# An elementwise GELU on one core: the first two loads put ahead of SyncE's register set-up

## Chip, cores, metric

The kernel runs on one core of one Trainium2 chip. The metric is device microseconds of the whole execution. Executions within 1.5% of the fastest of the same kernel count as fast.

## The reference

```python
# x, y: float32 [1024, 4096]
z = x + y
return 0.5 * z * (1 + np.tanh(np.sqrt(2 / np.pi) * (z + 0.044715 * z ** 3)))
```

33.55 MB are read and 16.78 MB written, with a handful of elementwise operations for each element.

## The kernel before

x and y come in four pairs of loads of 4 MB each, all issued by SyncE (SP below). GpSimd (POOL) and VectorE (DVE) add, ScalarE (ACT) squares and takes the sigmoid, VectorE multiplies, and three stores leave by the same queue. What matters here is the head of the program. Ahead of the kernel's body stands a head block in which each engine sets up its registers and all of them meet at a barrier. The kernel edits this block after its own schedule is made: it takes the first two loads out of the body and puts them ahead of SyncE's drain at the barrier, so that they need not wait for it.

```python
def begin_early(nc, count):
    blocks = nc.main_func.blocks
    head, body = blocks[0], blocks[1]
    SP = mybir.EngineType.SP
    queue = [i for i in body.instructions if i.engine == SP]
    moved = [i for i in queue if isinstance(i, mybir.InstDMACopy)][:count]
    assert not any(i.sync_info and i.sync_info.on_wait for i in moved)
    at = next(k for k, i in enumerate(head.instructions) if i.engine == SP and isinstance(i, mybir.InstDrain))
    for k, i in enumerate(moved):
        body.instructions.remove(i)
        head.instructions.insert(at + k, i)

# ... (at the end of the kernel)
    ctx.close()
    tc.close()
    tc.compile()
    begin_early(nc, 2)
    wait_late(nc)
```

`wait_late` edits the end of the program and is the same in both kernels. After these edits the launch code finishes the program in one more pass over all instructions, and hands it to the compiler. At the time of the edit the SyncE part of the head reads: a register set to zero, a base address loaded into two registers, four registers of bounds, [the two loads], drain, barrier, branch.

Of the kernel before, what the change touches and what calls it, by code (L numbers as in the profile page):

```python
# [10 lines left out]
def begin_early(nc, count):  # L11


    blocks = nc.main_func.blocks
    head, body = blocks[0], blocks[1]
    SP = mybir.EngineType.SP
    queue = [i for i in body.instructions if i.engine == SP]
    moved = [i for i in queue if isinstance(i, mybir.InstDMACopy)][:count]
    assert not any(i.sync_info and i.sync_info.on_wait for i in moved)
    at = next(k for k, i in enumerate(head.instructions) if i.engine == SP and isinstance(i, mybir.InstDrain))  # L20
    for k, i in enumerate(moved):
        body.instructions.remove(i)
        head.instructions.insert(at + k, i)


def wait_late(nc):
# [43 lines left out]
def kernel(  # L70
# [159 lines left out]
# [5 lines that stand above are left out]
# [29 lines left out]
```

## Time and profile before

| | before |
|---|---|
| time, median of the first 3 runs | 120.31 us (120.29 to 120.60) |
| span of the profiled run (120.49 us) | 118.8 us |
| DMA queue's share of 16 engines | 98.7% |
| busiest compute engine | VectorE, 62% |

The span runs from the first recorded instruction to the last. The zero of a profile's clock is therefore that first instruction, whichever it is. "SPq" is SyncE's sequencer; the duration of a DMA row there is the issue, not the transfer (0.38 us for the first load). The lines themselves stand in the prediction.

### The profile page before, as it was taken

The numbers are of one execution on the slowest core, as the hardware profiler recorded it, in microseconds if no ns is written. First come the engines' busy times: TensorE is split into PE (matmuls) and PEld (weight loads), VectorE is DVE, ScalarE is ACT, GpSimd is POOL, SyncE is SP. The second block draws the span as 40 slices with busy tenths as digits, with TensorE's granted clock in tenths as the row PEclk, the third lists the DMA queues.
The fourth block names the chain that finished last, engine by engine and source line by source line (L and its number), as shares of the span: only waits on it lengthen the run. The fifth ranks groups of instructions, "written<-read, shape, count | busy, mean of one in ns | idle before, by whom it ended". The sixth has DMA issues, their size and how long they took to land.

```text
span 118.8 us, 172 instructions
## 1 busy us (share of the span) xinstructions
DVE 73.7 (62%) x35; ACT 61.0 (51%) x34; POOL 69.7 (59%) x19
## 2 busy tenths in 40 slices
DVE  0000000635799995739999968999994999990000
ACT  5000000063888965197698647888839779810000
POOL 0000000699996099999959999959999990000000
DMA  7989898989999898989899898998899889999996
GB/s 243 463 375 507 353 529 353 507 375 474 408 419 463 375 507 353 518 364 496 386 452 430 386 496 353 529 529 353 353 596 463 353 353 441 441 441 441 397 397 265
DMA packets 1584, 50.33 MB, mean 424 GB/s; under 512 B 176, under 2 KB 176, under 8 KB 176
## 3 DMA queue, kind: packets, MB, share of 16 engines
q1 hardware_dynamic: 1584, 50.33, 98.7%
HBM read 33.55 MB, written 16.78 MB: 424 GB/s over the span
## 4 chain that ended last, share of the span: by engine, by line
DMA 51%; POOL 26%; POOLq 4%; DVE 4%; DVEq 2%; ACT 2%; issue 0%; SPq 0%
DMA y<-in_y_dram 51%; POOL z L153 26%; POOLq L231 4%; DVE w L164 2%; DVEq L231 2%; DVE z L176 2%; ACT w L158 2%; SPq L129 0%; POOLq L153 0%
## 5 line engine op out<-in xcount | busy, mean ns | idle before, releaser
L153 POOL TENSOR_TENSOR z<-z,y 128x2048 f32<-128x2048 f32 x15 | 69.4, 4660 | 28.3 <-DMA y<-in_y_dram 28.3
L158 ACT ACTIVATE w<-z 128x2048 f32<-128x2048 f32 x16 | 30.1, 1882 | 37.7 <-DVE z L153 21.5
L164 DVE SCALAR_TENSOR_TENSOR w<-w,z 128x2048 f32<-128x2048 f32 x16 | 36.7, 2296 | 11.2 <-ACT w L158 11.0
L176 DVE TENSOR_TENSOR z<-w,z 128x2048 f32<-128x2048 f32 (+1 forms) x17 | 35.9, 2155 | 0.0
L169 ACT ACTIVATE w<-w 128x2048 f32<-128x2048 f32 x16 | 29.7, 1855 | 4.4 <-DVE w L164 4.3
L153 DVE TENSOR_TENSOR z<-z,y 128x2048 f32<-128x2048 f32 x1 | 2.3, 2293 | 20.5 <-DMA y<-in_y_dram 20.5
L216 ACT ACT_TABLE_LOAD x1 | 1.3, 1283 | 1.3 <-PEq L248 1.3
L215 DVE MEMSET one<- 128x1 f32 x1 | 0.1, 59 | 1.3 <-PEq L248 1.3
L248 POOL MEMSET const-float32-0.0<- 128x1 f32 x1 | 0.1, 98 | 0.2 <-issue 0.2
L216 ACT ACTIVATE one<-one 128x1 f32<-128x1 f32 x1 | 0.2, 203 | 0.0
L248 POOL MEMSET const-bfloat16-1.0<- 128x1 bf16 x1 | 0.1, 101 | 0.0
L248 POOL MEMSET const-uint8-127<- 128x1 uint8 x1 | 0.1, 101 | 0.0
L248 POOL MEMSET const-float32-1.0<- 128x1 f32 x1 | 0.1, 98 | 0.0
## 6 DMA issues: line engine op xcount, KB each, us to landing
z<-in_x_dram SPq DMA_DIRECT2D x4, 4096.0 KB, 31.4
y<-in_y_dram SPq DMA_DIRECT2D x4, 4096.0 KB, 22.2
out_dram<-z SPq DMA_DIRECT2D x1, 5120.0 KB, 15.8
out_dram<-z SPq DMA_DIRECT2D x1, 3072.0 KB, 11.9
out_dram<-z SPq DMA_DIRECT2D x1, 22.0
```

What stands on the lines that cost most here:

```text
L153: eng.tensor_add(out=zt[:, a:b], in0=zt[:, a:b], in1=yt[s][:, o : o + b - a])
L158: nc.scalar.activation(out=wt[c], in_=zt[:, a:b], func=act.Square, scale=root)
L164: nc.vector.scalar_tensor_tensor(out=wt[c], in0=wt[c], scalar=c1, in1=zt[:, a:b], op0=alu.add, op1=alu.mult)
L169: nc.scalar.activation(out=wt[c], in_=wt[c], func=act.Sigmoid)
L176: ins = nc.vector.tensor_mul(out=zt[:, a + o : a + o + n], in0=wt[c][:, o : o + n], in1=zt[:, a + o : a + o + n],)
L215: nc.vector.memset(one, 0.0)
L216: nc.scalar.activation(out=one, in_=one, func=act.Sigmoid)
L231: tc.compile()
L248: nc = _bacc.Bacc("TRN2", target_bir_lowering=False, num_devices=1)
```

## The change

The intent: nothing at all should stand ahead of the two loads on SyncE. They use no register, as a new assertion makes sure, so they need not wait for the register set-up.

```diff
 def begin_early(nc, count):
-    blocks = nc.main_func.blocks
-    head, body = blocks[0], blocks[1]
+    head, body = (b.instructions for b in nc.main_func.blocks[:2])
     SP = mybir.EngineType.SP
-    queue = [i for i in body.instructions if i.engine == SP]
-    moved = [i for i in queue if isinstance(i, mybir.InstDMACopy)][:count]
+    moved = [i for i in body if i.engine == SP and isinstance(i, mybir.InstDMACopy)][:count]
     assert not any(i.sync_info and i.sync_info.on_wait for i in moved)
-    at = next(k for k, i in enumerate(head.instructions) if i.engine == SP and isinstance(i, mybir.InstDrain))
+    assert all(i.regs_accessed() == ((), ()) for i in moved)
+    at = next(k for k, i in enumerate(head) if i.engine == SP)
     for k, i in enumerate(moved):
-        body.instructions.remove(i)
-        head.instructions.insert(at + k, i)
+        body.remove(i)
+        head.insert(at + k, i)
```

## The prediction

Its sum came to 0 instructions removed and 0 added, 0.00 us, and so to the time of before. The 0.4 us of the intent now rest on the second estimate alone, 6 x 60 ns = 0.36 us.

> **What bounds the kernel now.** I read the page top down: busy shares, slices, DMA queue, then the chain of waits, the SyncE rows of the timeline, and SyncE's waits. The page first:
>
> ```profile
> span 118.8 us, 172 instructions
> DVE 73.7 (62%) x35; ACT 61.0 (51%) x34; POOL 69.7 (59%) x19
> ...
> DMA  7989898989999898989899898998899889999996
> GB/s 243 463 375 507 353 529 353 507 375 474 408 419 463 375 507 353 518 364 496 386 452 430 386 496 353 529 529 353 353 596 463 353 353 441 441 441 441 397 397 265
> ...
> q1 hardware_dynamic: 1584, 50.33, 98.7%
> HBM read 33.55 MB, written 16.78 MB: 424 GB/s over the span
> ```
>
> No compute engine is busy for more than 62% of the span. The DMA engines are: the one queue's packets take 98.7% of what 16 engines could give, and every slice between the first and the last has a DMA digit of 8 or 9. 50.33 MB over 118.8 us is the 424 GB/s of the last line. So this kernel is a transfer of a fixed 50.33 MB, and its length is: how late the transfer starts, plus bytes over rate, plus the end. The change aims at the first of the three. The first slice is visibly the thinnest of the early ones, 243 against 463 GB/s; in slices of 118.8/40 = 2.97 us that is some (463 - 243)/463 x 2.97 = 1.4 us of transfer missing at the start (an estimate, since neighbouring slices swing between 353 and 529).
>
> The chain of waits, which the page gives by line and another answer by time, begins so:
>
> ```profile
> 1.20 0.07 issue
> 1.26 0.33 SPq L129
> 1.59 0.05 issue
> 1.64 39.62 DMA y<-in_y_dram
> ```
>
> It starts not at the first pair of loads but at the second, issued at 1.26 and 1.64 us; the fourth load of the queue takes 39.62 us from issue to landing because it stands behind the 12 MB before it. These two issues come after the barrier of the kernel's head, and they are early enough: they queue behind the 8 MB of the first pair. So it is the first pair that sets when the queue begins to move. The beginning of the timeline:
>
> ```profile
> 0.00 0.38 SPq L129 DMA_DIRECT2D z<-in_x_dram  x1
> 0.23 0.10 POOL L248 MEMSET const-float32-0.0<- 128x1 f32 x1 [0.23 <-issue]
> ...
> 0.43 0.42 SPq L136 DMA_DIRECT2D y<-in_y_dram  x1
> 1.26 1.28 ACT L216 ACT_TABLE_LOAD   x1 [1.26 <-PEq L248]
> 1.26 0.33 SPq L129 DMA_DIRECT2D z<-in_x_dram  x1
> 1.33 0.06 DVE L215 MEMSET one<- 128x1 f32 x1 [1.33 <-PEq L248]
> 1.64 0.48 SPq L136 DMA_DIRECT2D y<-in_y_dram  x1
> ```
>
> This is the row to look at: the load of x is the first thing in the span, at 0.00. Nothing recorded of any engine is ahead of it, neither a SyncE instruction nor Pool's first constant at 0.23 us. In SyncE's list of waits no wait precedes either load; its first is of 0.2 us on the barrier:
>
> ```profile
> SPq L248 <- PEq L248: 0.2, 1, 0.2
> ```
>
> The profile does not show everything that is on the clock: the profiled run took 120.49 us and its span is 118.80, so 1.69 us of the time are outside the span. If instructions of SyncE ran unrecorded ahead of its first load, they would be in that part.
>
> [...] the first issue shows 0.38 us, while the median landing of x is 31.4 us after its issue. [...] No row of the trace shows a register instruction[...].
>
> **The change, part by part.** At the time when the kernel edits its own instruction list, the head of SyncE reads: a register set to zero, a base address loaded into two registers, four registers of bounds set, then the two loads (placed there already by the kernel before), then a drain and a wait of the barrier. The new code puts the two loads ahead of the six set-up instructions; an added assertion says that the loads use no register. The two loads' own waits, semaphores, sizes and order stay. Nothing else is added, removed or moved.
>
> What those six would cost if they ran, as estimates. [...] From the trace instead: SyncE's small instructions at the end of the kernel follow one another at about 60 ns (starts at 111.58, 111.64, 111.71 and 111.76 us), so 6 x 60 = 0.36 us. All of it would be on the path, since the queue would start that much earlier and is full ever after. So the intent is worth 0.4 us in 120.3, 0.3%.
>
> But I also built both kernels and compared what comes out. The instruction list is finished after the kernel's edits, and in the finished program of the kernel before, SyncE has no register set-up any more: its 30 instructions are 11 DMA issues, 13 semaphore instructions, 4 drains and 2 branches. The set-up is dropped as unused in both kernels. Engine by engine, the two programs are the same instructions in the same order, and the five engines' binary streams are the same byte for byte; only line numbers in the debug information differ, as the function is one line shorter. The trace of before fits: it has 28 records of SyncE, 11 DMA issues, 13 semaphore instructions and 4 drains, which is the finished list without its branches. So the cost removed is 0 instructions x anything = 0. Added: 0. The sum is 0.00 us, and the prediction is the time of before within its scatter.
>
> **The rivals.** First, the intent as written: the set-up runs and the loads overtake it; 0.4 us gained, about 119.9 us. For it: the 1.69 us outside the span, in which unrecorded instructions could lie. Against it: the finished program has none of them. Even if the whole 1.69 us were set-up, the time would be 118.6 us, 1.4% less and still within 2%.
>
> Second, something that SyncE needs is now not set when the first loads are issued, and they run slower, or with another split over the engines. For it: only that the source puts them ahead of a base load. Against: the same bytes are issued from the same place in the binary. It would cost time in proportion to 8 MB of 50, if at all; I give it almost nothing.
>
> Third, the loads do start earlier but the gain is hidden: the barrier ends at 1.2 us anyway, and the second pair waits for it. This would give 0 as well, but by a wrong reason: with the queue at 98.7% the first pair's start, not the barrier, sets the end.
>
> Fourth, another chip or another placement of the tensors: this moves the same program by its scatter. Three runs of before lie between 120.29 and 120.60, 0.26%, and the profiled one at 120.49.
>
> **Range and chances.** The middle is the median of before, 120.31; I say 120.33, a little above, because the runs scatter upwards (two at 120.3, one at 120.6, one at 120.49). The range is 119.95 to 120.75: it allows for somewhat more than the scatter seen on each side, and its lower end just takes in the first rival. Over 2% faster would need 117.9 us, more than all that is outside the span; over 2% slower 122.7 us, seven times the scatter. I give each 1%, and 98% to the same.
>
> **What would show it.** Right: a span near 118.8 us with the load of x at 0.00, the load of y at about 0.43 and the second pair at about 1.26 and 1.64 us; 172 instructions, again 28 of SyncE; 98 to 99% of the queue; a time outside the span of again 1.5 to 1.8 us. The distances inside the head are the test: with an identical binary they can move by some tens of ns alone. Wrong: if Pool's first constant or the barrier stood later relative to the load of x by 0.3 us or more, SyncE's first load would have moved against the other engines, so there was a set-up to overtake, and the first rival holds; if the first loads' landing times grew by more than a microsecond, the second does. And a repeated run of both on one chip that differs by more than 0.5% between the medians would say that identical streams are not all that decides.

## The result

The changed kernel takes 120.36 us (median of 6, 120.32 to 120.44), the kernel before 120.39 us (median of 6 runs, 120.29 to 120.60). The ratio is 0.9997, with a 95% interval of 0.9984 to 1.001: the same. Here and below a ratio compares the fast runs of the two kernels in the same rounds; it is not quite the ratio of the medians.

The page of the changed kernel:

```profile
span 118.8 us, 172 instructions
...
q1 hardware_dynamic: 1584, 50.33, 98.8%
HBM read 33.55 MB, written 16.78 MB: 424 GB/s over the span
```

Its chain of waits by time (start us, us, what), the first pieces:

```profile
1.20 0.07 issue
1.26 0.33 SPq L128
1.59 0.05 issue
1.64 39.59 DMA y<-in_y_dram
```

Its timeline, from the start:

```profile
0.00 0.38 SPq L128 DMA_DIRECT2D z<-in_x_dram  x1
0.23 0.10 POOL L247 MEMSET const-float32-0.0<- 128x1 f32 x1 [0.23 <-issue]
...
0.43 0.42 SPq L135 DMA_DIRECT2D y<-in_y_dram  x1
1.26 1.28 ACT L215 ACT_TABLE_LOAD   x1 [1.26 <-PEq L247]
1.26 0.33 SPq L128 DMA_DIRECT2D z<-in_x_dram  x1
...
1.64 0.49 SPq L135 DMA_DIRECT2D y<-in_y_dram  x1
```

Line by line these are the rows of before, one source line further up. The load of x is at 0.00, Pool's first constant 0.23 us behind it, the second pair at 1.26 and 1.64 us, and there are again 172 instructions. The distance between SyncE's first load and Pool's first constant is the one to look at. They are on two engines that wait for nothing before, so if the load had overtaken some set-up, Pool's row would now stand later. It has not moved by 0.01 us. For scale: in the traces of before, of the changed kernel and of its repetition below, Pool's constant stands at 0.23 us and the second load of x at 1.26 us each time, and the third load of x at 2.17, 2.18 and 2.21 us.

### The profile page after: what moved, and what is told of

Its sections match the earlier page's. It is cut to its first block, busy times and chain, and to the rows that moved or that the text cites. A ratio compares the mean times of both kernels' runs of the same rounds, so it can differ in the third digit from the quotient of the medians.

```text
span 118.8 us, 172 instructions
## 1 busy us (share of the span) xinstructions
DVE 73.7 (62%) x35; ACT 61.0 (51%) x34; POOL 69.6 (59%) x19
## 4 chain that ended last, share of the span: by engine, by line
DMA 51%; POOL 26%; POOLq 4%; DVE 4%; DVEq 2%; ACT 2%; issue 0%; SPq 0%
DMA y<-in_y_dram 51%; POOL z L152 26%; POOLq L230 4%; DVE w L163 2%; DVEq L230 2%; DVE z L175 2%; ACT w L157 2%; SPq L128 0%; POOLq L152 0%
```

## The experiments

Two questions are left: why is the change empty, and would it do what it was meant to if there were a set-up to overtake? The expectations name three theories.

- Theory A: the set-up is dropped when the program is finished, so there is nothing to overtake.
- Theory B, the intent: the set-up ran in the kernel before, and the loads now overtake it.
- Theory C: the barrier, and not the first pair of loads, sets the end, so that the order ahead of it is hidden.

The measure used throughout is the start of the first load less the start of Pool's first constant. The span's own zero cannot serve, since it moves when SyncE has recorded instructions ahead of its first load.

### The changed kernel again

The same file under another label.

> The changed kernel once more, against before on the same chip. Theory A (the set-up is dropped when the program is finished, so the binary streams are identical): ratio 1.000, within 0.2%, load of x at 0.00 and Pool's first constant at 0.23 us. Theory B (the set-up ran and was overtaken): 0.4 us faster, ratio 0.997, and Pool's constant 0.3 us or more later relative to the load of x.

Measured: 120.41 us (6 runs; one of them at 120.95) against 120.39 us, ratio 1.001 (0.9995 to 1.0024). The load of x is at 0.00 us and Pool's constant at 0.23 us. Two times over, then, there is no difference, and 0.4 us less (0.997) lies outside both intervals.

### The set-up kept, loads behind it (the order of before)

```diff
+def keep_setup(nc):
+    head, body = (b.instructions for b in nc.main_func.blocks[:2])
+    SP = mybir.EngineType.SP
+    setup = [i for i in head if i.engine == SP][:6]
+    regs = [r for i in setup for r in i.outs]
+    assert len(regs) == 7
+    issues = [k for k, i in enumerate(body) if i.engine == SP and isinstance(i, mybir.InstDMACopy)]
+    for r in regs:
+        nc.sync.keepalive_nop([r])          # "this register is still needed"; leaves no code
+        body.insert(issues[4] + 1, nc.cur_bb.bb.instructions.pop())
+
     tc.compile()
+    keep_setup(nc)
     begin_early(nc, 2)
```

The finished program now has SyncE's six set-up instructions ahead of the two loads, and is otherwise that of before.

> The order of before, with SyncE's six set-up instructions kept in the program (their results are named as needed by an empty instruction in the body, which itself leaves no code). Theory A: now there is something ahead of the first load, so about 0.36 us slower (estimate, 6 x 60 ns[...]), ratio 1.001 to 1.005; in the trace Pool's first constant moves from 0.23 us to about -0.1 us relative to the load of x. Theory B (before already paid for them): same as before, 120.4 us, Pool's constant still at +0.23 us. Theory C (the barrier and not the first pair sets the end, so that the order in the head is hidden): same time, with the loads later in the head.

Measured: 120.76 us (5 runs, 120.69 to 120.78) against 120.39 us, ratio 1.0029 (1.0017 to 1.0041). First the page's top line and the rows of its timeline:

```profile
span 119.0 us, 178 instructions
```

```profile
0.25 0.10 POOL L261 MEMSET const-float32-0.0<- 128x1 f32 x1 [0.25 <-issue]
...
0.38 0.38 SPq L141 DMA_DIRECT2D z<-in_x_dram  x1
...
1.63 0.33 SPq L141 DMA_DIRECT2D z<-in_x_dram  x1
```

Then all instructions of the head's source line (engine, operation, count, ns min/median/max, first and last start), of which two rows are new:

```profile
L261 SPq MOVE  x5: 29/29/40, 0.0 to 0.3; - x5
L261 SPq BASE_LOAD  x1: 12/12/12, 0.1 to 0.1; - x1
...
L261 SPq DRAIN  x1: 122/122/122, 1.3 to 1.3; - x1
L261 SPq EVENT_SEMAPHORE  x1: 17/17/17, 1.6 to 1.6; - x1
```

The same view of the kernel before has only these two rows for SyncE:

```profile
L248 SPq DRAIN  x1: 125/125/125, 0.9 to 0.9; - x1
L248 SPq EVENT_SEMAPHORE  x1: 17/17/17, 1.2 to 1.2; - x1
```

This settles theory B. Register moves and the base load are recorded when they run (the count goes from 172 to 178), and the kernel before has no record of them. The load of x now stands at 0.38 - 0.25 = 0.13 us, against -0.23 us before, so 0.36 us later. The medians differ by 120.76 - 120.39 = 0.37 us. So the set-up, where it exists, is paid in full.

### The set-up kept, loads ahead of it (the order of the change)

The edit of the run above, on the changed kernel.

> The order of the change, with the six set-up instructions kept: loads first, set-up behind them, then the barrier. Theory A: 120.4 us, ratio 1.000 to before, since the first pair starts at the same moment and the second pair, about 0.36 us later, queues behind 8 MB anyway. Theory B: the same as the changed kernel, also 1.000. Theory C: 0.36 us slower, as the barrier is later by the set-up.

Measured: 120.38 us (5 runs) against 120.39 us, ratio 0.9998 (0.9986 to 1.001). The timeline, and the row of the moves from the view by source line:

```profile
0.00 0.38 SPq L140 DMA_DIRECT2D z<-in_x_dram  x1
0.23 0.10 POOL L260 MEMSET const-float32-0.0<- 128x1 f32 x1 [0.23 <-issue]
...
1.53 0.34 SPq L140 DMA_DIRECT2D z<-in_x_dram  x1
```

```profile
L260 SPq MOVE  x5: 29/29/40, 0.9 to 1.2; - x5
```

With a set-up that survives, the change does what it was meant to. Between this kernel and the last there is nothing but the change, and it brings 120.76 - 120.38 = 0.38 us. The moves now stand at 0.9 to 1.2 us, and they make the barrier and the second pair 0.27 us later (1.53 against 1.26), which costs nothing. Theory C expected it to cost 0.36 us.

### Forty moves ahead of the loads

```diff
+def moves(nc, count, behind):
+    head, body = (b.instructions for b in nc.main_func.blocks[:2])
+    at = behind + ...   # place of the first early load in the head
+    for n in range(count):
+        nc.sync.reg_mov(nc.sync.alloc_register(f"m{n}"), 100 + n)
+        ...             # kept as above, placed in the head at `at`
+
     begin_early(nc, 2)
+    moves(nc, 40, 0)
```

> Forty register moves kept ahead of the two early loads, to have the effect large enough to read. Theory A: slower by 40 times a move[...], with the whole of it in the end of the last store. Theory C: less than half of the delay that the head shows.

A range is cut there, since no trace shows its lower end; its upper end was 40 x 60 ns = 2.4 us, ratio 1.020, from the 60 ns of the prediction's second estimate.

Measured: 122.49 us (4 runs, 122.47 to 122.51) against 120.39 us, ratio 1.0174 (1.0161 to 1.0187). The moves and the first rows:

```profile
L76 SPq MOVE  x40: 29/29/40, 0.0 to 2.0; - x40
```

```profile
0.25 0.10 POOL L263 MEMSET const-float32-0.0<- 128x1 f32 x1 [0.25 <-issue]
...
2.12 0.38 SPq L143 DMA_DIRECT2D z<-in_x_dram  x1
```

The first load is 1.87 + 0.23 = 2.10 us later, and the time is 2.10 us longer. A move is recorded as 29 ns, but one follows the other after 2.12 us / 40 = 53 ns: the recorded duration is about half of what it costs the sequencer.

### Forty moves behind the loads

The same on the changed kernel, with `moves(nc, 40, 2)`: between the two loads and the barrier.

> The forty register moves behind the two early loads, so between them and the barrier. The run with the moves in front took 122.49 us and its moves 52 ns each. Theory A: the first pair is back at the start, so 120.4 us, ratio 1.000 within 0.2%, although barrier and second pair come some 2.1 us later than in before (second pair near 3.3 us). Theory C (the barrier's time counts too): up to 2.1 us slower.

Measured: 120.41 us (6 runs, 120.26 to 120.71) against 120.36 us, ratio 0.9998 (0.9978 to 1.0018).

```profile
0.00 0.38 SPq L142 DMA_DIRECT2D z<-in_x_dram  x1
0.23 0.10 POOL L262 MEMSET const-float32-0.0<- 128x1 f32 x1 [0.23 <-issue]
...
3.26 0.33 SPq L142 DMA_DIRECT2D z<-in_x_dram  x1
```

Barrier and second pair come 2.00 us later than in before, and the time doesn't change: by the interval, any loss is at most 0.2 us. The queue still has most of the first 8 MB to move at 3.26 us (it moved 273 GB/s, 0.8 MB, in the first 3 us); the adds that need them begin at 21.9 us in the kernel before. The same forty instructions cost 2.10 us on one side of two issues and nothing that the runs can tell on the other.

### No early load

The kernel before without the call of `begin_early`.

> The kernel before without any early load: both wait for the barrier of the head. SyncE then comes to the barrier at once, Pool's drain at some 0.5 us is the last, and the first load goes out about 0.7 us later than in before, counted from Pool's constants (estimate from the rows of the trace of before). Theory A: 0.7 us slower, ratio 1.006. Theory C: same time.

Measured: 121.10 us (median of 6, 121.01 to 121.64) against 120.36 us, ratio 1.0057 (1.0036 to 1.0079).

```profile
0.24 0.10 POOL L247 MEMSET const-float32-0.0<- 128x1 f32 x1 [0.24 <-issue]
...
0.74 0.37 SPq L129 DMA_DIRECT2D z<-in_x_dram  x1
```

The first load is at 0.50 us after Pool's constant, so 0.73 us later, and the time is 0.74 us longer. This is what the kernel before had already gained by its own edit.

### Only the load of x early

`begin_early(nc, 1)` on the kernel before.

> Only the load of x early, the load of y behind the barrier. Theory A: the queue has 4 MB, some 10 us, from the same moment, so 120.4 us, ratio 1.000, although the load of y is issued some 0.4 us later. Theory C: a change of the barrier's place (some 0.4 us earlier) shows as up to 0.4 us faster.

Measured: 120.41 us (6 runs) against 120.36 us, ratio 0.9994 (0.9976 to 1.0011). In the timeline the load of x stays at 0.00 with Pool's constant at 0.23 us; the load of y is issued at 0.79 instead of 0.43 us. Of the first pair it is the load of x alone that has to be early: its 4 MB keep the queue busy far beyond 0.79 us (in the kernel before it has landed at 12.1 us).

### A better head, first try: the first load split by rows

```diff
-        nc.sync.dma_start(out=zt[:, a:b], in_=xv[:, a:b])
+        for f, e in ((0, 16), (16, P)) if i == 0 else ((0, P),):
+            nc.sync.dma_start(out=zt[f:e, a:b], in_=xv[f:e, a:b])
...
-    begin_early(nc, 2)
+    begin_early(nc, 3)
```

> Looking for a better head: the changed kernel with the first load in two, rows 0 to 15 alone first and then the other 112. If the 0.62 us from the end of the first issue to the first packet stays and the shorter issue ends sooner, packets begin up to 0.3 us sooner and the time is up to 0.3 us less, ratio 0.9975; if an issue costs the same whatever its rows, or 16 rows don't fill the engines until the second part comes, it is the same or up to 0.3 us slower.

Measured: 130.20 us (6 runs) against 120.36 us, ratio 1.0794 (1.077 to 1.0818). This is a miss: no branch of the expectation allowed for more than 0.3 us. The two parts of the first load on its page (KB, us from issue to landing):

```profile
z<-in_x_dram SPq DMA_DIRECT2D x1, 3584.0 KB, 21.6
...
z<-in_x_dram SPq DMA_DIRECT2D x1, 512.0 KB, 7.5
```

The stretches (us, busy times of DVE, ACT and POOL, clock, DMA share, GB/s) of it and then of the kernel before:

```profile
0.00:10.00 10.00, 0.06 (x1) 1.49 (x2) 0.20 (x4) 1.00 0.95 170
10.00:20.00 10.00, 0.00 (x0) 0.00 (x0) 0.00 (x0) 1.00 1.03 269
```

```profile
0.00:10.00 10.00, 0.06 (x1) 1.49 (x2) 0.20 (x4) 1.00 0.91 367
10.00:20.00 10.00, 0.00 (x0) 0.00 (x0) 0.00 (x0) 1.00 1.05 452
```

The part of 112 rows is issued at 0.44 us and so has landed at 22.0 us; in before the whole first load has landed at 12.1 us. That is 9.9 us later, so the 9.8 us are lost within this one load. The DMA engines count as busy (0.95, 1.03), yet move 170 and 269 GB/s. The issue of 16 rows takes 0.39 us, as that of 128 rows does (0.38), and the first packet starts at 1.03 us, not earlier than the 1.00 us of before. So the 9.8 us are slow packets, not a late start.

The packet records of the trace show two parts. The first sixteen 32 KB packets, the 16 rows, took 2.8 to 4.3 us each (median 3.87), where the first sixteen of before took 1.2 to 2.1 us (1.83); the last of them ends at 5.9 us against 3.3, so 2.6 us are lost there. The 112 packets that follow took 1.7 to 3.9 us (median 2.19) against 1.21 in before, and the last ends at 21.0 us against 11.8. Of those 9.2 us, then, the larger part, some 6.6 us, is lost in the load of 112 rows.

No run here shows why the packets of either part are slow, and this stays open. What is shown is the warning: here, splitting one load by rows cost 9.8 us, far more than the head has to give (the early loads gained 0.74 us in it).

### A better head, second try: the first load split by columns

As above, with 1,024 columns of all rows first and the other 7,168 behind.

> The first load in two again, but by columns: 1,024 columns of all 128 rows first, then the other 7,168. It tells whether the 10 us that the split by rows cost lie in the rows or in having one more DMA. If in the rows: packets of full length stay near 1.21 us as in before, and the time is 120.4 us, ratio within 0.3% of 1.000, perhaps 0.1 us slower for the later load of y; if in the extra DMA: again several us slower. The first packet starts at 1.0 us if it follows the issue (whose 128 rows are the same), sooner if the smaller pieces matter.

Measured: 120.30 us (6 runs, 120.22 to 120.63) against 120.41 us, ratio 0.9994 (0.998 to 1.0008). Its first stretch, in the same form as above:

```profile
0.00:10.00 10.00, 0.06 (x1) 1.49 (x2) 0.20 (x4) 1.00 0.92 374
```

One DMA more costs nothing that the runs can tell, so what cost 10 us was the split by rows. The first packet starts at 1.01 us again, 0.63 us after the end of the first issue, though it is only 4 KB long: neither fewer rows nor shorter pieces brought it forward. By the interval a gain, if there is one, is at most 0.2%. No version tried beats the two kernels.

### The runs on one line each

Starts are taken from the timelines above, against Pool's first constant, and less those of before (-0.23 us for the load of x, 1.03 us for the second pair). "Time" is the difference of the medians to before in the same rounds.

| kernel | first load later by | second pair later by | time |
|---|---|---|---|
| changed | 0.00 us | 0.00 us | -0.03 us |
| set-up kept, ahead of the loads | 0.36 | 0.35 | +0.37 |
| set-up kept, behind the loads | 0.00 | 0.27 | -0.01 |
| 40 moves ahead | 2.10 | 2.10 | +2.10 |
| 40 moves behind | 0.00 | 2.00 | +0.05 |
| no early load | 0.73 | 0.37 | +0.74 |
| only x early | 0.00 | -0.09 | +0.05 |

The first column gives the last, one to one, over a range of 0.36 to 2.10 us. The second has no part in it that the runs can tell: 2.00 us of it are worth at most 0.2 us by the interval.

## Why the prediction was right

That the time would be the same is the weaker part of it: the intent, had it been real, was worth 0.3%, which is "same" too. What was right is the mechanism, and the set-up runs show it.

- **The bound.** It said that a full queue makes the length "how late the transfer starts, plus bytes over rate, plus the end", and that the first pair, not the barrier, decides the start. The table shows just that.
- **The change as zero.** It said that the finished programs are identical, because the set-up is dropped as unused in both. The trace agrees: no moves in either, the same 172 instructions, the same distances. The comparison of the two builds itself is in none of the runs. That use decides it was only inferred from one build; the kernel with the registers named as needed shows it, since the six instructions came back by that alone.
- **The first rival** (the set-up runs and is overtaken) fell, but the prediction left it more room than it deserved. It thought that unrecorded set-up could lie in the 1.69 us between time and span. The run with the set-up kept shows that register moves are recorded and lie inside the span. With that known, the trace of before excludes them: SyncE's first record there is the load. The prediction could not know it from the traces it had; its build comparison carried the point.
- **The second rival** (loads run slower without the base address) fell: with the base load really behind the loads, the result was correct and the time 120.38 us.
- **The third rival** (gain hidden by the barrier) was rightly rejected; 40 moves behind the loads made the barrier 2.00 us later and cost nothing that the runs can tell.
- **The fourth rival** (another chip) came to nothing: on the three chips of the experiments the medians of before are 120.39, 120.36 and 120.41 us.
- **The range.** Its lower end, 119.95 us, was said to take in the first rival, which had been put at about 119.9 us. It does so only with the gain of 0.36 us (120.31 - 0.36 = 119.95), not with the rounded 0.4. The time alone was thus a weak test at that end; the distances in the head were the real one.
- **The size of the intent.** The estimate from the trace for six instructions (60 ns each, 0.36 us) was right in the sum: the measured delay is 0.36 to 0.37 us. Luck has a part in that, since the 60 ns came from semaphore instructions and drains: a move takes 53 ns and the base load about twice as much. Of the 0.38 us from the first set-up instruction to the first load, five moves leave 0.38 - 5 x 0.053 = 0.11 us for the base load (an estimate; recorded are 12 ns).

## What to carry to other kernels

Before a reordering is counted as a gain, look at the finished program and at the records of the trace: an instruction that the last pass drops can't be overtaken, and the change is then no change at all (172 records in both kernels here, 178 with the set-up kept). In this kernel, whose DMA queue is busy for 98.7% of the span, what stood ahead of the first load was paid in the end one for one (0.36 to 2.10 us), and what stood between it and the later loads, while the queue was full, was not (2.00 us, to within 0.2 us). Measure such starts against an instruction of another engine, since the span's zero is the first recorded instruction and moves with the thing measured (with the set-up kept ahead, the first load stands at 0.38 us instead of 0.00).
